# Keeping the first loads in the written order, and adding the last w_down tiles to r in SBUF

## The chip, the cores and the metric

One core of one Trainium2 chip runs the kernel. The metric is the device time of one execution in microseconds (us), as the median of several runs. Beside it stands one profiled execution, whose span (first to last instruction) is a little shorter than its device time.

## The reference

One decoder layer on 256 tokens and 2048 channels, all in fp32. Cut to what matters here:

```python
h = rms_norm(r, g_mix);  z = h @ w_in                      # 2048 -> 3072 (q, k, v) + 3072 (conv) + 4096 (gates)
q, k, v = split(z)                                         # 8 heads of 128, q and k normalised per head
attn = softmax(causal(q k^T)) v;  y_attn = attn @ w_attn_out
y_conv = (c_b * conv3(c_c * c_x)) @ w_conv_out
r = r + (sigmoid(g_a) * y_attn + sigmoid(g_c) * y_conv) @ w_o
r = r + relu(rms_norm(r, g_mlp) @ w_up)**2 @ w_down        # 2048 -> 8192 -> 2048
r = r + sigmoid(rms_norm(r, g_ple) @ w_ple_gate) * (p @ w_ple_proj)
```

## The kernel before, in words

Every weight is read once from DRAM in fp32 and split by ScalarE (ACT) and VectorE (DVE) into a high and a low part (`w_hi`, `w_lo`), as the activations are; three products of parts (high by high, high by low, low by high) on TensorE (PE) make one fp32 product. All 277 MB of weights go through this, so the kernel is one long row of products on PE with splits ahead of it and loads ahead of the splits.

The stages, in order of time:

- **The first chunks** (`first_chunks`): q, k and v of heads 0 to 3. The sum over 2048 channels goes in 16 steps of 128; in each step 256 KB of weights for each of q, k and v (`raw_first`) and 128 KB of x (loaded in pairs of steps, 256 KB) come in, are split, and enter 18 products of 512 columns. This function is written out in its order of work: `ordered[0] = True` marks each of its instructions, the loads too, to be kept in program order on its engine.
- **The second q, k, v chunk** (`rows(qkv(1), ...)` and so on, tiles `raw`): four units of 1 MB for each of q, k, v, and 24 products for each. After each unit one entry of the list `pending` is run (`run_pending`). The attention of head 0 to 7 is put there in four stages each: transposes of q and k (`tr_qk`), scores and softmax, transposes of the probabilities, values.
- **conv, gates, branches, w_o**, then **up and down** (96 units `g`): 64 units of w_up and 32 of w_down. Half of w_down's output goes through the loop's own products (`ps_dn`), the other half through a scheme of seven products per block (`P1` to `P7`).
- **The gate** (`ps_pg`), 16 tiles, with the projection of p.

The order of the instructions on each engine comes from a scheduler that runs when the kernel is built. An instruction that is not kept in program order may be put ahead of others as soon as its buffer is free. The loads of the second q chunk (`raw`, four buffers) are not kept in order. All these loads are issued by SyncE (SP), with at most eight DMAs of SP and ACT under way: each waits for the eighth one before it, and the load of the vector `vec` from ACT's queue is one of the eight.

The residual r lies in SBUF only until the norm ahead of up is taken; a copy in DRAM (`r_kept`, eight tiles of two column blocks) is kept, and GpSimd (POOL) adds the finished tiles of `ps_dn` to it by DMAs that accumulate (`dn_done`, two for each tile `n`, both into the same block, so that the second waits for the first). Towards the end r is loaded back by `load_r`. The last four tiles of w_down (`n` of 12 to 15 with `q` 3) are added by DVE in SBUF. In unit 95 ACT takes r in blocks 10 to 14 into the gate's input (`enter_high`), and only behind them on ACT stand the copies out of the banks `P1` and `ps_dn` (tiles `p1` and `dn`); the copy `dn` frees the bank that the first gate product needs.

Of the kernel before, what the change touches and what calls it, by code (L numbers as in the profile page):

```python
# [12 lines left out]
ALU = mybir.AluOpType  # L13
# [6 lines left out]
S = 256  # L20
# [18 lines left out]
def hybrid_block_kernel(ctx: ExitStack, tc: tile.TileContext, ins: dict, out: bass.AP):  # L39
# [9 lines left out]
    nc = tc.nc  # L49
# [8 lines left out]
    def slot(shape, dtype, name):  # L58
        return bp.tile(shape, dtype, tag="slot", name=name)
# [4 lines left out]
    def psum(kind, shape, name):  # L64
        i = banks[kind].pop(0)
        banks[kind].append(i)
        return pp.tile(shape, F32, tag=f"b{i}", name=name)

    def bank(name):
        return psum("acc", [P, CW], name)  # L70


    ordered = [False]

    def inorder(ins):
        return tc.keep_in_program_order(ins) if ordered[0] else ins

    def act(*args, **kw):
        return inorder(nc.scalar.activation(*args, **kw))  # L79

    def mm(*args, **kw):
        return inorder(nc.tensor.matmul(*args, **kw))  # L82

    def load(*args):
        return inorder(nc.sync.dma_start(*args))

    class vec_ops:
        def __getattr__(self, name):
# [29 lines left out]
    def rsqrt_mean(dst, sumsq, n, k):  # L118

        dve.tensor_scalar(dst, sumsq, 1.0 / n, EPS, op0=ALU.mult, op1=ALU.add)  # L120
        nc.gpsimd.tensor_tensor(dst, dst, half[:, :k], op=ALU.pow)
# [23 lines left out]
    pending = []  # L145

    def run_pending(n):
        for _ in range(min(n, len(pending))):
            pending.pop(0)()
# [37 lines left out]
    def rows(units, xs, name, pops=1):  # L187

        nu = len(units)
        ps = [bank(f"ps_{name}_{t}") for t in range(NT)]  # L190
        for u, unit in enumerate(units):
            wt = unit()
            for j in range(KU):
                k = KU * u + j
                hi, lo = (p[:, (j % 2) * CW:(j % 2 + 1) * CW] for p in wt[j // 2])
                for t in range(NT):
                    xh, xl = (xs[k][:, i, t * P:(t + 1) * P] for i in range(2))
                    mm(ps[t], xh, hi, start=k == 0, stop=False)
                    mm(ps[t], xh, lo, start=False, stop=False)
                    mm(ps[t], xl, hi, start=False, stop=k == KU * nu - 1)  # L200
            run_pending(pops)
        return ps

    def qkv(c, loader=load_unit):
        return [lambda u=u: loader(ins["w_qkv"][c, u]) for u in range(4)]
# [60 lines left out]
    def rstd_rows(rstd, name):  # L266
        diag = slot([P, NT, P], F32, f"diag_{name}")
        for t in range(NT):
            dve.tensor_scalar_mul(diag[:, t, :], ident, rstd[:, t:t + 1])
        ps = psum("tr", [P, S], f"ps_rstd_{name}")  # L270
        mm(ps, ones, diag.rearrange("p t s -> p (t s)"), start=True, stop=True)
        row = const.tile([P, S], F32, tag="rstd_row", name=f"rstd_row_{name}")
        act(row, ps, AF.Copy)
        return row


    xT, st0, xraw = {}, {}, {}
# [76 lines left out]
    qs, ks, vs = {}, {}, {}  # L354

    def tokens(ps, name):

        parts = []
        for t in range(NT):
            raw = slot([P, CW], F32, f"{name}_{t}")  # L360
            act(raw, ps[t], AF.Copy, scale=st0["col"][:, t:t + 1])
            parts.append(raw)
        return parts

    def qk_evac(ps, name):
        parts = tokens(ps, name)
        ssq = sm.tile([P, NT, 4], F32, tag="ssqh", name=f"ssq_{name}")
        for t in range(NT):
            junk = sm.tile([P, HD], F32, tag="junk", name="junk", bufs=1)
            for h in range(4):  # L370
                act(junk, parts[t][:, h * HD:(h + 1) * HD], AF.Square, accum_out=ssq[:, t, h:h + 1])
        rinv = sm.tile([P, NT, 4, 1], F32, tag="rinvh", name=f"rinv_{name}")
        rsqrt_mean(rinv.rearrange("p t h o -> p (t h o)"), ssq.rearrange("p t h -> p (t h)"), HD, NT * 4)
        for t in range(NT):
            heads = parts[t].rearrange("p (h d) -> p h d", d=HD)
            dve.tensor_mul(heads, heads, rinv[:, t].to_broadcast([P, 4, HD]))
        return parts
# [51 lines left out]
    for c in range(2):  # L429
        if c == 0:  # L430
            ps_q, ps_k, ps_v = first_chunks((0, 2, 4), ("q0", "k0", "v0"))
            qs[c], ks[c] = qk_evac(ps_q, "q0"), qk_evac(ps_k, "k0")
            vs[c] = tokens(ps_v, "v0")
        else:
            qs[c] = qk_evac(rows(qkv(1), xT, "q1"), "q1")
            ks[c] = qk_evac(rows(qkv(3), xT, "k1"), "k1")
            vs[c] = tokens(rows(qkv(5), xT, "v1"), "v1")
        for h in range(4 * c, 4 * c + 4):
            head(h)
        if c == 0:  # L440
            pending.insert(4, lambda: st0.update(row=rstd_rows(st0["col"], "mix")))


    w_in = ins["w_in"]
# [2 lines left out]
    for j in range(8):  # L447
# [5 lines left out]
        u = slot([P, S + 2], F32, f"u_{j}")  # L453
# [27 lines left out]
    for c in range(4):  # L481
        gates = []
        for i in range(2):
            ps = rows(tiles("w_in", 24 + 16 * i + 4 * c), xT, f"g{i}_{c}", pops=2)
            g = [slot([P, CW], F32, f"g{i}_{c}_{t}") for t in range(NT)]
# [14 lines left out]
    r = {}  # L500

    def add_to_r(n, src):

        dst = r[n // 2][:, n % 2, :]
        for i in range(2):
            dve.tensor_add(dst, src[:, i * S:(i + 1) * S], dst)
# [6 lines left out]
    r_kept = [dram.tile([P, 2, S], F32, tag=f"r{u}", name=f"r_kept_{u}") for u in range(8)]  # L513
# [43 lines left out]
    def stages(g):  # L557
        return staged[g] if 0 <= g < len(staged) else ()
# [131 lines left out]
    def up_sum(k, st):  # L690
        a = u_raw[k] = temp("a")
        dve.tensor_add(a, st[:, :S], st[:, S:])
        dve.scalar_tensor_tensor(a, a, 0.0, row1, op0=ALU.max, op1=ALU.mult)
# [27 lines left out]

    def dn_done(q, n, st):
        if q < 3 or n < 12:
            for i in range(2):
                nc.gpsimd.dma_start(r_kept[n // 2][:, n % 2, :], st[:, i * S:(i + 1) * S], accum_op=ALU.add)  # L725
        else:
            add_to_r(n, st)

    def load_r(u):
        r[u] = slot([P, 2, S], F32, f"r_{u}")  # L730
        nc.gpsimd.dma_start(r[u], r_kept[u])
# [7 lines left out]
    for g in range(NU):  # L739
        kind, i = units[g]  # L740
        ordered[0] = g > 1
        if g == 5:
            banks["acc"] = [7]
        load_raw(g + 3)
        for j, x in stages(g + 2):
            if x == 0:
                load_pair(j)
        for u in {88: (6, 7), 90: (0, 1), 91: (4,), 92: (2, 3), 93: (5,)}.get(g, ()):
            load_r(u)
        if g == 93:  # L750
            ss2 = slot([P, 2, S], F32, "ss2")
        if g == 94:
            praw = slot([P, 2, S], F32, "p")
            load(praw, ins["pT"].rearrange("p (k s) -> p k s", s=S))
        xs = hT if kind == "up" else {k: uT[16 * i[0] + k] for k in range(16)}
        ps = cols(wU[g][1:], xs, f"{kind}_{g}")
        if g == 0:
            rstd1 = rstd_columns(ss1, "mlp")
        if g == 1:
            row1 = rstd_rows(rstd1, "mlp")  # L760
        done = [n for n in range(g) if n in evac] if g > 1 else []
        ups = [units[n][1] for n in done if units[n][0] == "up"]
        on_act, on_dve = unit_half(g + 2, 0)
        on_act()
        for n in done:
            if units[n][0] == "up":
                up_sum(units[n][1], evac.pop(n))
        on_dve()
        for k in ups:
            up_high(k)  # L770
        for k in ups:
            up_low(k)
        for n in done:
            if units[n][0] == "dn":
                dn_done(*units[n][1], evac.pop(n))
        make_stages(stages(g))
        for work in unit_half(g + 2, 1):
            work()
        entering = {94: (8, 9), 95: (10, 11, 12, 13, 14)}.get(g, ())
        for n in entering:  # L780
            enter_high(n)
            if n % 2 == 1:
                square(n // 2)
        if g == NU - 1:
            p1 = evacuated(prod["P1"], "p1")
        for n in entering:
            enter_low(n)
        if g == NU - 1:
            d, e = (slot([P, CW], F32, n) for n in "de")
            dve.tensor_sub(d, p1, prod["P5"])  # L790
            dve.tensor_add(e, d, prod["P3"])
        evac[g] = evacuated(ps, kind)
        if kind == "up" and i == 63:
            up_sum(i, evac.pop(g))
            up_high(i)
            up_low(i)
        for j, x in stages(g - 1):
            products(j, x)
# [186 lines left out]
```

## Time and profile before

| | |
|---|---|
| device time, median of 3 runs | 1460.81 us (1459.35 to 1461.93) |
| the profiled execution, device time | 1459.0 us |
| its span | 1457.2 us |
| PE busy | 1439.0 us, 99% of the span |
| DVE busy | 1057.6 us, 73% |
| ACT busy | 822.4 us, 56% |
| POOL busy | 70.3 us, 5% |
| moved by DMA | 289.95 MB, mean 199 GB/s |
| mean granted TensorE clock | 0.999 of full speed |

1.8 us of the profiled execution lie outside its span. A busy PE is not always one at its full rate: its matmuls overlap, their ends are modelled, and the clock can be granted at half.

### The profile page before, as it was taken

Reading aid. Unit: us, or ns where it says so; the run is one execution under the profiler, and the core shown is the slowest. Engines: PE = TensorE matmul, PEld = TensorE weight load, DVE = VectorE, ACT = ScalarE, POOL = GpSimd, SP = SyncE. Lnnn points to the kernel's source line nnn. Section 1 sums busy time; section 2 is a strip of 40 time slices with the busy share of each in tenths; the row PEclk is TensorE's granted clock in tenths of the full one; section 3 lists DMA queues with packets and bytes.
Section 4 is the critical chain, followed back from the end, with each engine's and each line's share of the span. In section 5 each row is a group of like instructions: output and inputs, shape, how many; then the busy total and the mean of one; then the engine's idle time right before and its main releaser. Section 6 shows DMA issues by size and latency. Waiting matters only on the chain.

```text
span 1457.2 us, 19838 instructions
## 1 busy us (share of the span) xinstructions
PE 1439.0 (99%) x7553; PEld 1235.7 (85%) x7553; DVE 1057.6 (73%) x1616; ACT 822.4 (56%) x1291; POOL 70.3 (5%) x99
## 2 busy tenths in 40 slices
PE   7999999999999999999999999999999999999998
PEld 5878888888888888888888888888888888887887
DVE  5755677755555646676889788887888879987984
ACT  4766555554444444445666566665666556655752
POOL 0010000000000000000001100021000200011000
PEclk9999999999999999999999999999999999999999
DMA  9755554555555666563658865697557866578470
GB/s 299 248 176 174 173 174 174 173 190 194 195 183 194 201 213 225 202 216 126 229 178 229 214 218 181 198 238 222 190 181 225 238 183 220 198 229 238 150 248 22
DMA packets 139375, 289.95 MB, mean 199 GB/s; under 512 B 8208, under 2 KB 83216, under 8 KB 119056
## 3 DMA queue, kind: packets, MB, share of 16 engines
q1 hardware_dynamic: 129792, 277.11, 57.0%
q0 software_dynamic: 9344, 11.54, 4.7%
q8 instruction: 59, 0.97, 0.3%
q14 instruction: 36, 0.29, 0.1%
q10 hardware_dynamic: 144, 0.04, 0.0%
HBM read 277.12 MB, written 11.53 MB: 198 GB/s over the span
## 4 chain that ended last, share of the span: by engine, by line
PE 96%; ACT 1%; DMA 1%; DVE 1%; issue 0%; POOL 0%; SPq 0%; DVEq 0%; ACTq 0%
PE ps_up L82 24%; PE ps_g L82 12%; PE ps_dn L82 12%; PE P L82 10%; PE ps_conv L82 9%; PE ps_o L82 6%; PE ps_pg L82 6%; PE ps_y L82 6%; PE ps_q L82 3%; PE ps_k L82 3%; PE ps_v L82 3%; PE ps_proj L82 1%; DMA x<-in_xT_dram 1%; DMA r<-r_kept 0%; ACT w_hi L79 0%; PE tr L470 0%
## 5 line engine op out<-in xcount | busy, mean ns | idle before, releaser
L89 DVE TENSOR_TENSOR w_lo<-raw,w_hi 128x1024 fp32r<-128x1024 f32 (+1 forms) x524 | 529.0, 1026 | 233.4 <-ACT w_hi L79 170.4
L79 ACT ACTIVATE w_hi<-raw 128x1024 fp32r<-128x1024 f32 (+1 forms) x524 | 459.2, 895 | 216.1 <-PE ps_g L82 62.0
L82 PE MATMUL ps_up<-x,w_hi 128*128 128x512 f32 x1024 | 254.5, 391 | 0.4 <-ACT up L79 0.4
L82 PEld LDWEIGHTS ps_up<-x,w_hi 128*128 128x128 f32 x1024 | 191.1, 188 | 40.5 <-ACT up L79 3.6
L82 PE MATMUL ps_g<-w_hi,x 128*128 128x512 f32 x512 | 159.1, 390 | 0.0
L82 PEld LDWEIGHTS ps_up<-x,w_lo 128*128 128x128 f32 x1024 | 131.3, 191 | 5.0
L82 PE MATMUL ps_up<-x,w_lo 128*128 128x256 f32 x1024 | 132.8, 283 | 0.0
L82 PE MATMUL ps_dn<-x,w_hi 128*128 128x512 f32 x512 | 126.8, 390 | 0.0
L82 PEld LDWEIGHTS ps_g<-w_hi,x 128*128 128x128 f32 x512 | 96.2, 188 | 19.8
L82 PEld LDWEIGHTS ps_dn<-x,w_hi 128*128 128x128 f32 x512 | 96.2, 188 | 18.9 <-ACT dn L79 0.3
L79 ACT ACTIVATE t_hi<-t 128x1024 fp32r<-128x1024 f32 x64 | 67.5, 1054 | 72.2 <-DVE t L89 72.2
L79 ACT ACTIVATE up<-ps_up 128x512 f32<-128x512 f32 x64 | 38.2, 597 | 119.2 <-PE ps_up L82 119.1
L82 PE MATMUL ps_g<-w_lo,x 128*128 128x512 f32 x256 | 99.7, 389 | 0.0
L82 PE MATMUL ps_conv<-x,w_hi 128*128 128x512 f32 x384 | 97.9, 398 | 0.0
L89 DVE TENSOR_TENSOR t_lo<-t,t_hi 128x1024 fp32r<-128x1024 f32 x64 | 78.1, 1220 | 16.7 <-ACT t_hi L79 16.7
L82 PEld LDWEIGHTS ps_conv<-x,w_hi 128*128 128x128 f32 x384 | 70.9, 189 | 13.3
L82 PE MATMUL ps_y<-w_hi,x 128*128 128x512 f32 x256 | 79.5, 389 | 0.0
L725 POOL DMA_DIRECT2D r_kept<-dn x56 | 48.4, 887 | 523.0 <-ACT dn L79 376.9
L82 PE MATMUL ps_pg<-x,w_hi 128*128 128x512 f32 (+1 forms) x272 | 68.1, 383 | 3.2 <-ACT dn L79 3.2
L82 PE MATMUL P<-t_hi,s 128*128 128x512 f32 x192 | 70.6, 395 | 0.0
L82 PEld LDWEIGHTS ps_dn<-x,w_lo 128*128 128x128 f32 x512 | 65.7, 191 | 2.5
L82 PE MATMUL ps_dn<-x,w_lo 128*128 128x256 f32 x512 | 66.4, 283 | 0.0
(206 smaller groups left out, 2133.9 us busy)
## 6 DMA issues: line engine op xcount, KB each, us to landing
raw<-in_w_up_dram SPq DMA_DIRECT2D x64, 1024.0 KB, 5.3
raw<-in_w_in_dram SPq DMA_DIRECT2D x56, 1024.0 KB, 5.0
raw_s<-in_w_down_dram SPq DMA_DIRECT2D x128, 256.0 KB, 4.3
raw<-in_w_down_dram SPq DMA_DIRECT2D x32, 1024.0 KB, 5.1
raw<-in_w_branch_dram SPq DMA_DIRECT2D x16, 1024.0 KB, 5.1
raw<-in_w_o_dram SPq DMA_DIRECT2D x16, 1024.0 KB, 4.9
raw<-in_w_qkv_dram SPq DMA_DIRECT2D x12, 1024.0 KB, 5.0
raw_first<-in_w_qkv_dram SPq DMA_DIRECT2D x48, 256.0 KB, 7.2
```

Source lines behind the costliest of these rows:

```text
L79: return inorder(nc.scalar.activation(*args, **kw))
L82: return inorder(nc.tensor.matmul(*args, **kw))
L89: return lambda *args, **kw: inorder(getattr(nc.vector, name)(*args, **kw))
L725: nc.gpsimd.dma_start(r_kept[n // 2][:, n % 2, :], st[:, i * S:(i + 1) * S], accum_op=ALU.add)
```

## The change

Two things. First, loads are also kept in program order until the four units of the second q chunk have been written (`ordered_loads`), and an entry that does nothing is put ahead of the attention's first stage in `pending`, so that all stages are run one unit later. Second, the DMAs that add the tiles 8 to 11 of the last quarter of w_down accumulate into the tile r in SBUF instead of `r_kept`, and r's blocks 4 to 7 are loaded back ahead of them, in unit 88.

```diff
+    ordered_loads = [True]
+
     def load(*args):
-        return inorder(nc.sync.dma_start(*args))
+        dma = nc.sync.dma_start(*args)
+        return tc.keep_in_program_order(dma) if ordered[0] or ordered_loads[0] else dma
...
-            qs[c] = qk_evac(rows(qkv(1), xT, "q1"), "q1")
+            ps_q = rows(qkv(1), xT, "q1")
+            ordered_loads[0] = False
+            qs[c] = qk_evac(ps_q, "q1")
...
-            pending.insert(4, lambda: st0.update(row=rstd_rows(st0["col"], "mix")))
+            pending.insert(0, lambda: None)
+            pending.insert(5, lambda: st0.update(row=rstd_rows(st0["col"], "mix")))
...
     def dn_done(q, n, st):
         if q < 3 or n < 12:
+            to = r_kept if q < 3 else r
             for i in range(2):
-                nc.gpsimd.dma_start(r_kept[n // 2][:, n % 2, :], st[:, i * S:(i + 1) * S], accum_op=ALU.add)
+                nc.gpsimd.dma_start(to[n // 2][:, n % 2, :], st[:, i * S:(i + 1) * S], accum_op=ALU.add)
...
-        for u in {88: (6, 7), 90: (0, 1), 91: (4,), 92: (2, 3), 93: (5,)}.get(g, ()):
+        for u in {88: (4, 5, 6, 7), 91: (0, 1), 92: (2, 3)}.get(g, ()):
             load_r(u)
```

SP, the queue that issues the loads, at the start of the program, before and then after. `raw` are units of the second q chunk (1 MB), `raw_first` and `x_0` pieces of the first step (256 KB and 128 KB):

```order
L85 DMA raw_783<-in_w_qkv_dram 128x2048
L85 DMA raw_825<-in_w_qkv_dram 128x2048
L85 DMA raw_873<-in_w_qkv_dram 128x2048
L85 DMA raw_first_114<-in_w_qkv_dram 128x512
L85 DMA x_0_116<-in_xT_dram 128x256
L85 DMA raw_first_118<-in_w_qkv_dram 128x512
```

```order
L88 DMA raw_first_114<-in_w_qkv_dram 128x512
L88 DMA x_0_116<-in_xT_dram 128x256
L88 DMA raw_first_118<-in_w_qkv_dram 128x512
L88 DMA raw_first_120<-in_w_qkv_dram 128x512
L88 DMA x_0_116<-in_xT_dram 128x256
```

The three units of 1 MB have left the head of the queue, and a fourth its middle; all four now stand right behind the last `raw_first`, and behind the second chunk's twelve units SP's rows are the same as before.

PE in the second q chunk, at the first of the attention's stages, before and then after (`ps_q` are the products of the chunk, `tr_qk` the transposes of q and k of head 0):

```order
L82 MATMUL ps_q_1_782<-w_hi,x 128x512
L389 MATMUL tr_qk_817<-ident,q_0_737 128x128
L389 MATMUL tr_qk_817<-ident,q_1_739 128x128
L82 MATMUL ps_q_0_781<-w_hi,x 128x512
L389 MATMUL tr_qk_817<-ident,k_0_757 128x128
```

```order
L82 MATMUL ps_q_1_782<-w_hi,x 128x512
L393 MATMUL tr_qk_851<-ident,q_0_737 128x128
L393 MATMUL tr_qk_851<-ident,q_1_739 128x128
L393 MATMUL tr_qk_851<-ident,k_0_757 128x128
L393 MATMUL tr_qk_851<-ident,k_1_759 128x128
```

Before, the transposes stood behind the first 24 products of the chunk, now they stand behind 48.

POOL from unit 88 to 93, before and then after (`r_kept` is the copy in DRAM, `r_4` to `r_7` the tiles in SBUF, `dn` a finished tile of w_down):

```order
L731 DMA r_6_11730<-r_kept_6_4733 128x512
L731 DMA r_7_11732<-r_kept_7_4734 128x512
L725 DMA r_kept_4_4731<-dn_11791 128x256 x2
L731 DMA r_0_11876<-r_kept_0_4727 128x512
L731 DMA r_1_11878<-r_kept_1_4728 128x512
L725 DMA r_kept_4_4731<-dn_11862 128x256 x2
L731 DMA r_4_11959<-r_kept_4_4731 128x512
L725 DMA r_kept_5_4732<-dn_11939 128x256 x2
L731 DMA r_2_12032<-r_kept_2_4729 128x512
L731 DMA r_3_12034<-r_kept_3_4730 128x512
L725 DMA r_kept_5_4732<-dn_12018 128x256 x2
L731 DMA r_5_12111<-r_kept_5_4732 128x512
```

```order
L739 DMA r_4_11730<-r_kept_4_4731 128x512
L739 DMA r_5_11732<-r_kept_5_4732 128x512
L739 DMA r_6_11734<-r_kept_6_4733 128x512
L739 DMA r_7_11736<-r_kept_7_4734 128x512
L733 DMA r_4_11730<-dn_11795 128x256 x2
L733 DMA r_4_11730<-dn_11866 128x256 x2
L739 DMA r_0_11959<-r_kept_0_4727 128x512
L739 DMA r_1_11961<-r_kept_1_4728 128x512
L733 DMA r_5_11732<-dn_11939 128x256 x2
L739 DMA r_2_12034<-r_kept_2_4729 128x512
L739 DMA r_3_12036<-r_kept_3_4730 128x512
L733 DMA r_5_11732<-dn_12020 128x256 x2
```

The load of `r_5` has moved from behind the accumulates into block 5 to ahead of all of them; the last of POOL's DMAs is now an accumulate.

## Rows read from the trace of the kernel before

**Rows 1.** Waits of PE over the whole span (us in total, times, longest):

```profile
PE ps_q L82 <- DVE x L89: 7.4, 1, 7.4
PE ps_pg L82 <- ACT dn L79: 3.2, 1, 3.2
PE tr_qk L389 <- DVE k L89: 1.7, 1, 1.7
```

**Rows 2.** Timeline, 0 to 40 us (start, length, engine, line, operation, [idle before, releaser]):

```profile
0.74 1.34 SPq L85 DMA_DIRECT2D raw<-in_w_qkv_dram  x3
1.19 4.02 PE L82 MATMUL idle<-zero 128*128 128x512 bf16 x9 [1.19 <-DVE half L89]
...
12.07 0.35 DVE L89 TENSOR_SCALAR x<-x,vec 128x256 fp32r<-128x256 f32 x1 [10.92 <-DMA x<-in_xT_dram]
...
12.57 1.19 PE L82 MATMUL ps_q<-w_hi,x 128*128 128x512 f32 x2 [7.36 <-DVE x L89]
...
17.61 0.63 PE L82 MATMUL ps_v<-w_hi,x 128*128 128x512 f32 x2
```

**Rows 3.** Chain that ended last, 0 to 160 us (start, length, what):

```profile
2.86 9.11 DMA x<-in_xT_dram
...
12.57 2.90 PE ps_q L82 x6
...
19.16 1.36 PE ps_q L82 x6
...
125.15 5.47 PE ps_k L82 x24
```

**Rows 4.** DMA view, issues of 0 to 2 us, then queues of 3 to 3.5 us:

```profile
vec<-in_vec_dram ACTq DMA_DIRECT2D x1, 37.0 KB, 5.4
...
q1 hardware_dynamic: 23, 0.19, 89.0%
q10 hardware_dynamic: 23, 0.01, 5.7%
```

**Rows 5.** Windows: length, busy time (instructions) per engine, granted clock, DMA share, GB/s:

```profile
5.21:12.57 7.36, 0.00 (x1) 0.03 (x1) 0.50 (x2) 0.63 (x1) 0.00 (x0) 1.00 1.01 379
19.16:64.04 44.88, 44.88 (x200) 37.18 (x199) 35.65 (x64) 32.70 (x61) 0.00 (x0) 1.00 0.96 295
155.00:1300.00 1145.00, 1144.55 (x6061) 986.87 (x6060) 846.07 (x1282) 644.85 (x960) 51.85 (x70) 1.00 0.63 199
1344.03:1347.22 3.19, 0.00 (x0) 0.00 (x0) 2.32 (x6) 3.14 (x7) 0.00 (x0) 1.00 0.00 0
1347.22:1353.00 5.78, 5.62 (x25) 4.76 (x26) 5.61 (x11) 1.98 (x3) 0.00 (x0) 0.70 0.00 0
```

**Rows 6.** Timeline of SP at the end of the first chunks:

```profile
53.34 5.47 SPq L85 DMA_DIRECT2D raw_first<-in_w_qkv_dram  x6
```

**Rows 7.** Timeline, second q and k chunk: PE's first product, DVE's softmax end, ACT's copies:

```profile
81.15 0.39 PE L82 MATMUL ps_q<-w_hi,x 128*128 128x512 f32 x1
...
128.33 0.55 DVE L89 TENSOR_SCALAR s<-s,den 128x128 f32<-128x128 f32 x2
...
131.99 1.26 ACT L79 ACTIVATE k<-ps_k,rstd_mix 128x512 f32<-128x512 f32 x2
```

**Rows 8.** Timeline of POOL, from 1280 us:

```profile
1288.44 0.88 POOL L725 DMA_DIRECT2D r_kept<-dn  x1 [22.15 <-ACT dn L79]
...
1294.50 1.44 POOL L731 DMA_DIRECT2D r<-r_kept  x2
...
1330.51 0.86 POOL L725 DMA_DIRECT2D r_kept<-dn  x1 [6.75 <-DMA r_kept<-dn]
1336.49 0.58 POOL L731 DMA_DIRECT2D r<-r_kept  x1 [5.12 <-DVE x L89]
```

**Rows 9.** Tile dn from 1270 us: landing of its eight accumulating DMAs:

```profile
DMA to landing us min/median/max: 3.6/7.2/8.0
```

**Rows 10.** Timeline of ACT, unit 95:

```profile
1335.64 2.00 ACT L79 ACTIVATE w_hi<-raw 128x1024 fp32r<-128x1024 f32 x2
1343.07 0.91 ACT L79 ACTIVATE x<-r,vec 128x256 fp32r<-128x256 f32 x2 [5.43 <-DMA r<-r_kept]
```

## The prediction

> **What bounds the kernel now.** I read first what PE waited for, since PE is busy 99% of the span: only three waits of any size stand there, 7.4 us before the first `ps_q`, 1.7 us at `tr_qk` and 3.2 us before `ps_pg` [rows 1]. Then the windows, to see whether time won early would be lost in the middle: from 155 to 1300 us PE is busy for 1144.55 of 1145.00 us [rows 5]. A late start or a late end cannot be made up there, and an early one is passed on, as long as loads and splits keep the pace that PE sets; the DMA engines are at 0.63 in that stretch. So each of the three waits counts in full, and the change touches all three. Then the timeline and the chain around each.
>
> At the start SP issues three units of 1 MB first, from 0.74 us on [rows 2]. The first piece of x is issued only at 2.86 us and lands 9.11 us later, at 11.97 us [rows 3]; DVE and PE start right on it, at 12.07 and 12.57 us [rows 2]. Between 5.21 and 12.57 us the DMA engines are full and move 379 GB/s, and PE does nothing [rows 5]. The reader is to see that this is data of a later stage: the second chunk's first product runs at 81.15 us [rows 7].
>
> At the end ACT waits 5.43 us for the load of r and takes x from it at 1343.07 us [rows 10]. POOL issued this load at 1336.49 us, after the accumulates into `r_kept` that must have landed before it, the last of them issued at 1330.51 us [rows 8]. Behind these instructions on ACT stands the copy `dn` that PE waits for.
>
> **The change part by part: the start.** It removes three transfers of 1.05 MB from the head of the queue: 3.15 MB at 379 GB/s [rows 5] are 8.3 us. The first x would land near 11.97 - 8.3 = 3.7 us. It needs `vec` too, whose load took 5.4 us from its issue at about 0.74 us, so until 6.1 us. That is an upper bound. In the half microsecond from 3 us its queue q10 and SP's q1 moved 23 packets each [rows 4], q1's packets of 0.19 MB / 23 = 8 KB: small packets and large ones took turns. With rows of 2 KB (256 KB over 128 rows) in place of 8 KB the turns are about a fourth as long, so I estimate `vec` by about 4.2 us. Then x is scaled (0.35 us [rows 2]) and is ready before the nine idle products end, at 1.19 + 4.02 = 5.21 us [rows 2]. I take the first real product at 5.2 us in place of 12.57; with `vec` at 6.1 us it would be 6.6 us.
>
> A second term lies in the pace. The first six products took 2.90 us (0.48 each), later six take 1.36 us (0.227 each) [rows 3]; the slow pairs last until about 17 us, and at 17.61 us a pair takes 0.63 us [rows 2]. The idle products ran at 4.02 / 9 = 0.45 us. So PE ran at the lower of its two levels (1.2 and 2.4 GHz) after standing still for 7.36 us, although the clock column reads 1.00 before it: the duration decides, not the column. The step of 18 products took from 12.57 to 19.16 us, 6.6 us in place of 3 x 1.36 = 4.1: 2.5 us lost. Now real products come straight behind 4.02 us of idle ones. The bounds are a loss of 0 and of 2.5 us; I take 0.4, near the first, because it was the pause that stood ahead of the slow stretch, and it goes. So step 1 would start at 5.2 + 4.1 + 0.4 = 9.7 us where it started at 19.16 [rows 3]: **9.4 us**. With `vec` late and the slow pace kept it is 6.6 + 6.6 = 13.2 us, a gain of 5.9; with no loss at all, 9.9.
>
> What hides the rest: a step brings 3 x 262 + 131 = 917 KB, at 295 GB/s [rows 5] in 3.1 us, and PE uses 4.1 us for it. ACT and DVE are busy for 32.70 and 35.65 of 44.88 us [rows 5], so they keep up too. The page "SBUF — State Buffer" of the Trainium skill, section "The DMA setup-cost knee", speaks against this change: each transfer pays a fixed cost, and one of 256 KiB reaches 224 GB/s where 1 MiB reaches 341. By that figure a step takes 917 / 224 = 4.1 us to load, just PE's own pace, and the first chunks would hang on the loads. The 295 GB/s with pieces of that size in flight say that they overlap, and decide.
>
> The four units of the second chunk lose their early start. SP issued the last piece of the first chunks at about 53.34 + 5.47 = 58.8 us [rows 6], now near 49.4. Four units are 4.19 MB, 14.2 us at 295 GB/s, so all have landed by 64 us and the first by some 54; PE needs the first at 81.15 - 9.4 = 71.8 us [rows 7]. The cover is over 15 us; if it were gone, the first unit's 3.6 us would be the price.
>
> **The transposes.** PE waited 1.7 us at `tr_qk` for the normalised k [rows 1]. One unit later means 24 products or 5.47 us later [rows 3], so 3.8 us remain to spare: **1.7 us**. All later stages of the attention slip by one unit. For head 1 the softmax now meets the copies of the second k. Before, DVE ended it at 128.33 + 0.55 = 128.9 us [rows 7], and PE's products covered until 125.15 + 5.47 = 130.6 [rows 3]: 1.7 us to spare. Two copies ahead of it take 1.26 us [rows 7]. It still fits; if it didn't, some tenths each.
>
> **The end.** Accumulating into r makes the load of `r_5` early and leaves an accumulate last. I follow POOL's new order from the first accumulate at 1288.44 us [rows 8]: the second of each tile waits for the first, which lands after 7.2 us [rows 9]; there are four such waits and the last landing, 5 x 7.2 = 36 us, and between them three issues of 0.88 us and two pairs of loads of 1.44 us [rows 8], 5.5 us. Block 5 is complete at 1330 us, with the longest landing, 8.0 us [rows 9], at 1334. No row shows an accumulate that ends in SBUF; loads of r and accumulates are the nearest, and I take the accumulates' own landing. ACT reaches block 5 at 1335.64 + 2.00 = 1337.6 us [rows 10], so the wait goes, and the copy `dn` comes before PE is done with the last `P`, at 1344.03 us. That gives 3.2 us [rows 5], and more: behind the pause the granted clock was 0.70 for 5.78 us [rows 5]. At two levels, 1.00 and 0.50, that is 0.6 x 5.78 = 3.5 us at half rate, 1.7 us lost, and 0.16 us more of PE idle lie there. Sum **5.0 us**; if DVE's chain behind it (additions from P1 to P7) holds PE up, 3.2. The four loads in unit 88 need buffers early; they stand ahead of the first accumulate, which waited 22.15 us idle [rows 8] for its tile, and that is their cover.
>
> On the landing: the page "DMA: Bandwidth & Descriptors" of the Trainium skill, section "Anatomy of one DMA", says that most of a transfer's fixed cost is the wait for the confirmed write, longest where it goes to HBM. By it the new accumulates land sooner than 7.2 us, and the slack of 7.6 us grows; no run here shows it yet, and the sum stays.
>
> **Sum.** 9.4 + 1.7 + 5.0 = 16.1 us. The profiled execution took 1459.0 us, which makes 1442.9; it lies 1.8 us under the median of the runs, 1460.8, which would make 1444.7. I say 1443.9, between the two.
>
> **Rivals.** (1) The first step stays slow, or `vec` is late: PE's pace does not care for the idle products. For it speaks that all of them ran slowly. The gain at the start is 7.3 (slow pace alone) to 5.9 us, the time 1446 to 1447.5. (2) Block 5 is late still: accumulates into SBUF of 9 us or more each. The end's 5 us are lost, 1449. (3) The start is given back: the first chunks hang on the loads, as the first page's figure has it, or the second chunk waits for its units. The start's 9.4 us shrink to 2 or so, 1451. Against it stand 295 GB/s and the 15 us of cover. (4) Slower: the chain of accumulates grows so long that PE waits longer than all that is won before. The load of r ended ACT's wait at 1343.07 us [rows 10]; adding 9.4 + 1.7 gives 1354.2 as the point from which it decides, so 12.1 us for each of the five landings: (1354.2 - 1288.44 - 5.5) / 5. At 13 us each the time would be 1464. The longest seen is 8.0 [rows 9]. (5) It does not do what it says: the first x lands as late as now, because the DMA engines start slowly and not because of the three units; then 1453 from the other two terms.
>
> **Chances.** My forecast 0.68, its own range 1441.5 to 1446. (1) 0.14, (2) 0.06, (3) 0.07, (4) 0.02, (5) 0.03. The range must leave out no more than 2 in 10: it reaches over the first two rivals to 1450, and down to 1441.0 for a start and end at their upper bounds. A measurement here can tell about 0.2%, 2.9 us, from no change. All cases but (4) win more than that: faster 0.95, same 0.03, slower 0.02.
>
> **What would show it.** In the profile after: the first `ps_q` at about 5 us, no pause between the idle products and it, the first 18 products in little over 4.1 us, the second chunk's first product near 72 us, no wait at `tr_qk`, the last accumulate landed well before ACT's x in unit 95, PE without a pause before `ps_pg` and a granted clock of 1.00 there. I am wrong if PE waits for `w_hi` or `x` in steps 1 to 4, if the first products take 0.48 us each, if a wait of PE on POOL's DMA remains at the end, or if pauses appear between 155 and 1300 us that weren't there.

## The result, and the profile after

The changed kernel took 1444.34 us (median of 4 runs, 1443.79 to 1445.12), the kernel before 1460.08 (4 runs, 1457.51 to 1461.93): a ratio of 0.9894, 95% interval 0.9877 to 0.9911. The forecast was 1443.9 us, within 1441.0 to 1450.0. The profiled execution after took 1445.12 us with a span of 1443.3, the one before 1459.0, so the two traces differ by 13.9 us where the medians differ by 15.7. All that follows explains the 13.9.

What PE waited for after (line, releaser; us in total, times, longest); [rows 1] are the three longest of the same list of before:

```profile
PE idle L82 <- DVE half L93: 1.2, 1, 1.2
PE ps_up L82 <- ACT up L79: 0.4, 1, 0.4
PE ps_rstd_mix L82 <- DVE diag_mix L93: 0.4, 1, 0.4
PE tr_qk L393 <- DVE k L93: 0.3, 1, 0.3
```

The three waits of before, 12.3 us, are gone but for 0.3 us at `tr_qk`, and a new one of 0.4 stands at `ps_rstd_mix`. (`ps_ss_mix` sums the squares of x for the first norm; `rstd_mix` is the norm's factor, begun on DVE and finished on POOL; `ps_rstd_mix` lays it out along a row.) To see where the time came from, I read from both timelines of PE when it starts the same product; the difference is the time won up to there.

| start of | before, us | after, us | won |
|---|---|---|---|
| first `ps_q` | 12.57 | 5.36 | 7.21 |
| step 1 of the first chunks | 19.00 | 10.23 | 8.77 |
| step 2 | 23.08 | 14.94 | 8.14 |
| `ps_ss_mix` (48 products before the end of the first chunks) | 69.32 | 61.18 | 8.14 |
| second chunk, first product | 81.15 | 73.01 | 8.14 |
| first `ps_g` (attention and conv are over) | 299.72 | 290.97 | 8.75 |
| last `ps_dn` | 1341.34 | 1332.70 | 8.64 |
| first `ps_pg` | 1347.22 | 1335.22 | 12.00 |
| `ps_ss_ple` | 1370.48 | 1356.61 | 13.87 |
| last product's end | 1453.04 | 1439.17 | 13.87 |

So the start brought 8.1 us, the stretch from the second chunk to the first `ps_g` 0.6, and the end 5.2; in between 0.1 was lost. The timeline of the start (start, length, engine, line, operation, idle before and releaser):

```profile
1.19 4.02 PE L82 MATMUL idle<-zero 128*128 128x512 bf16 x9 [1.19 <-DVE half L93]
5.36 1.19 PE L82 MATMUL ps_q<-w_hi,x 128*128 128x512 f32 x2
...
6.17 0.63 ACT L79 ACTIVATE w_hi<-raw_first 128x512 fp32r<-128x512 f32 x1 [1.30 <-DMA raw_first<-in_w_qkv_dram]
...
6.35 0.83 PE L82 MATMUL ps_q<-w_lo,x 128*128 128x512 f32 x2
...
7.02 0.63 PE L82 MATMUL ps_q<-w_hi,x 128*128 128x512 f32 x2
...
7.69 0.63 ACT L79 ACTIVATE w_hi<-raw_first 128x512 fp32r<-128x512 f32 x1 [0.89 <-DMA raw_first<-in_w_qkv_dram]
...
11.12 1.30 ACT L79 ACTIVATE w_hi<-raw_first 128x512 fp32r<-128x512 f32 x2 [1.61 <-DMA raw_first<-in_w_qkv_dram]
...
11.80 0.73 PE L82 MATMUL ps_k<-w_hi,x 128*128 128x512 f32 x2
...
12.53 0.73 PE L82 MATMUL ps_k<-w_lo,x 128*128 128x512 f32 x2
```

Read it against [rows 2]: the first real products stand directly behind the idle ones, and only two pairs are slow (1.19 and 0.83 us) before one takes 0.63. Step 0 takes 4.87 us where 18 products at full pace take 4.1. ACT waits for pieces of weights there, but PE does not: its products follow each other without a pause, so the slow pairs are the difference. Step 1 takes 4.71 us. There the piece of k's weights comes late, ACT waits for it until 11.12 us, and the products that use it start only at 11.80 and 12.53. In step 1 the loads hold PE, for 0.6 us.

Windows of after (length, busy time and instructions of PE, PEld, DVE, ACT, POOL, granted clock, DMA share, GB/s), for the first step, the stretch behind the first `ps_pg` and the middle:

```profile
5.21:9.70 4.49, 4.34 (x17) 3.57 (x17) 2.81 (x7) 1.90 (x3) 0.00 (x0) 1.00 0.93 260
1335.22:1341.00 5.78, 5.78 (x36) 5.05 (x35) 5.64 (x10) 2.84 (x6) 0.00 (x0) 1.00 0.02 4
155.00:1300.00 1145.00, 1144.56 (x6063) 986.46 (x6062) 850.23 (x1285) 644.77 (x958) 54.74 (x74) 1.00 0.63 201
```

The first row shows 260 GB/s at a share of 0.93: the DMA engines are nearly full. The second row answers to the last of [rows 5]: no pause ahead of it and a clock of 1.00 where it was 0.70. The third is the middle, as full as before.

The second chunk, from the timeline:

```profile
60.09 2.01 ACT L79 ACTIVATE w_hi<-raw 128x1024 fp32r<-128x1024 f32 x2 [1.41 <-DMA raw<-in_w_qkv_dram]
...
61.18 0.95 PE L82 MATMUL ps_ss_mix<-ones,ss 128*128 128x1 f32 x8
61.18 3.71 DVE L93 TENSOR_TENSOR w_lo<-raw,w_hi 128x1024 fp32r<-128x1024 f32 x3 [1.70 <-ACT w_hi L79]
...
64.81 0.15 DVE L93 TENSOR_SCALAR rstd_mix<-ps_ss_mix 128x2 f32<-128x2 f32 x1
64.88 1.22 DVE L93 TENSOR_TENSOR w_lo<-raw,w_hi 128x1024 fp32r<-128x1024 f32 x1
...
65.05 1.61 POOL L125 TENSOR_TENSOR rstd_mix<-rstd_mix,half 128x2 f32<-128x2 f32 x1 [62.58 <-DVE rstd_mix L93]
...
83.45 1.29 DVE L93 TENSOR_TENSOR k<-k,rinv_k 128x512 f32<-128x512 f32 x2 [1.53 <-POOL rinv_k L125]
...
84.90 0.30 PE L393 MATMUL tr_qk<-ident,k 128*128 128x128 f32 x1 [0.30 <-DVE k L93]
```

`ps_ss_mix` is done at 62.1 us, but DVE takes it up (`rstd_mix`) only at 64.81, since three splits of raw units stand ahead, and the first of these units landed late: ACT waited for it until 60.09. Everything up to the normalised k hangs on `rstd_mix`. Before, the three splits were done by the time `ps_ss_mix` was, and DVE took it up at once; the same two rows of DVE there:

```profile
70.31 0.16 DVE L89 TENSOR_SCALAR rstd_mix<-ps_ss_mix 128x2 f32<-128x2 f32 x1 [0.22 <-PE ps_ss_mix L82]
...
88.07 1.29 DVE L89 TENSOR_TENSOR k<-k,rinv_k 128x512 f32<-128x512 f32 x2 [1.53 <-POOL rinv_k L121]
```

The end, from the timelines of POOL, ACT and PE, and below it the landing of the eight accumulating DMAs (min, median, max):

```profile
1279.80 0.89 POOL L733 DMA_DIRECT2D r<-dn  x1 [16.26 <-ACT dn L79]
...
1312.74 0.88 POOL L733 DMA_DIRECT2D r<-dn  x1 [5.43 <-DMA r<-dn]
...
1328.89 0.89 ACT L79 ACTIVATE x<-r,vec 128x256 fp32r<-128x256 f32 x2
...
1335.22 1.52 PE L82 MATMUL ps_pg<-x,w_hi 128*128 128x512 f32 x6
```

```profile
DMA to landing us min/median/max: 3.5/6.2/7.8
```

The last accumulate is issued at 1312.74, so block 5 is complete near 1318.9 us; ACT comes to it at 1328.89 and waits for nothing. That is 10 us to spare. PE begins `ps_pg` straight behind the last `P`.

### The profile page after: what moved, and what is told of

Its sections match the earlier page's. It is cut to its first block, busy times and chain, and to the rows that moved or that the text cites. A ratio compares the mean times of both kernels' runs of the same rounds, so it can differ in the third digit from the quotient of the medians.

```text
span 1443.3 us, 19851 instructions
## 1 busy us (share of the span) xinstructions
PE 1436.6 (100%) x7553; PEld 1232.9 (85%) x7553; DVE 1057.8 (73%) x1616; ACT 822.4 (57%) x1291; POOL 71.2 (5%) x99
## 4 chain that ended last, share of the span: by engine, by line
PE 92%; DMA 4%; ACT 2%; DVE 1%; issue 0%; POOL 0%; SPq 0%; ACTq 0%; DVEq 0%; POOLq 0%
PE ps_up L82 24%; PE ps_dn L82 12%; PE ps_g L82 12%; PE P L82 11%; PE ps_conv L82 9%; PE ps_o L82 7%; PE ps_pg L82 6%; PE ps_y L82 6%; DMA raw_first<-in_w_qkv_dram 2%; PE ps_v L82 2%; DMA x<-in_xT_dram 1%; DMA raw<-in_w_qkv_dram 1%; PE ps_k L82 1%; PE ps_q L82 1%; PE ps_proj L82 1%; ACT w_hi L79 1%
## 5 line engine op out<-in xcount | busy, mean ns | idle before, releaser
L733 POOL DMA_DIRECT2D r_kept<-dn x48 | 41.1, 877 | 476.2 <-ACT dn L79 351.9
```

The costliest lines, as they stand in the source:

```text
L733: nc.gpsimd.dma_start(to[n // 2][:, n % 2, :], st[:, i * S:(i + 1) * S], accum_op=ALU.add)
```

## Experiments

Times are medians of the runs named. "Won at `ps_ss_mix`" and the like are differences of PE's starts against the profiled execution of before, as in the table above.

**Only the order of the loads**, on the kernel before:

```diff
+        dma = nc.sync.dma_start(*args)
+        return tc.keep_in_program_order(dma) if ordered[0] or ordered_loads[0] else dma
...
+            ps_q = rows(qkv(1), xT, "q1")
+            ordered_loads[0] = False
```

> Only the order of the loads is changed. Theory A (read from the trace after): the early start is worth 8.1 us up to the second chunk's first product, and then the raw units of the second chunk, which now land late, put the normalised k some 3.5 us late against PE; with the transposes still in their old place the wait at tr_qk grows from 1.7 to about 5 us. Net about 4.7 us faster than before, a profiled time near 1454. Rival B (the late units delay nothing that PE waits for; the small waits of the trace after come from the moved transposes): tr_qk stays at 1.7 us, net 8.1 us, near 1451. The end is as before in both: about 3.2 us of wait before ps_pg.

1455.33 us (8 runs, 1452.13 to 1456.66) beside 1460.03 of the kernel before (22 runs, 1454.70 to 1463.53), ratio 0.9965 (0.9951 to 0.9978). It won 9.0 us at `ps_ss_mix` and had 3.1 left at the first `ps_g`. Its two longest waits of PE, and its windows around and behind the first of them:

```profile
PE tr_qk L392 <- DVE k L92: 5.7, 1, 5.7
PE ps_pg L82 <- ACT dn L79: 3.0, 1, 3.0
```

```profile
81.00:84.00 3.00, 0.07 (x1) 0.10 (x2) 1.47 (x3) 0.26 (x1) 2.06 (x1) 0.56 0.83 292
84.00:87.00 3.00, 3.00 (x9) 2.31 (x10) 1.52 (x2) 0.84 (x2) 0.00 (x0) 0.50 0.38 115
87.00:90.00 3.00, 3.00 (x12) 2.43 (x11) 0.01 (x1) 1.06 (x1) 0.00 (x0) 0.80 0.79 317
```

Theory A holds, and its price was too low: the wait grew to 5.7 us, and PE, once it had stood still, came back at the lower level (a clock of 0.50, then 0.80 in a window that holds the rise), which costs some 2 us more. Alone, this part gives back two thirds of what it wins.

**Only the moved transposes**, on the kernel before:

```diff
-            pending.insert(4, lambda: st0.update(row=rstd_rows(st0["col"], "mix")))
+            pending.insert(0, lambda: None)
+            pending.insert(5, lambda: st0.update(row=rstd_rows(st0["col"], "mix")))
```

> Only the transposes of the first heads are moved by one unit. Theory A: the wait of 1.7 us at tr_qk goes and nothing comes in its place, since with the old order of loads the raw units land early and 3.8 us of cover remain: 1.7 us faster, profiled near 1457.3, PE waits at tr_qk and ps_rstd_mix of 0.1 us or less. Rival B: the move itself brings the waits of 0.3 us at tr_qk and 0.4 at ps_rstd_mix that the changed kernel shows: 1.0 us faster, with these two waits in PE's list.

1456.66 us (10 runs, 1452.25 to 1460.16), ratio 0.9984 (0.9968 to 0.9999). The wait at `tr_qk` is gone and `ps_rstd_mix` shows 0.4 us: half of each theory. The move itself brings the wait at `ps_rstd_mix`, and not the one at `tr_qk`. From `ps_ss_mix` to the first `ps_g` this kernel won 1.3 us (1.7 less 0.4); its first chunks ended 0.6 us later than before, so 0.7 are left there, and 1.8 at the end, where the wait before `ps_pg` was 2.5 us. By the ratio it won 2.3 us, hardly more than the scatter of these kernels. Its trace also holds a row that the one of before lacks, the granted clock at the start:

```profile
8.00:11.00 3.00, 0.00 (x0) 0.00 (x0) 0.00 (x0) 0.00 (x0) 0.00 (x0) 0.55 0.98 394
11.00:14.00 3.00, 1.44 (x4) 1.18 (x5) 1.67 (x4) 1.26 (x2) 0.00 (x0) 0.50 0.97 242
```

While PE stands and waits for x, the clock falls to the lower level, and the first products run at it. The prediction inferred this from durations, against a column that read 1.00.

**Loads and transposes, without the part on r:** both edits above.

> Order of the loads and place of the transposes, without the part on r. If the parts add up: 8.1 + 0.6 us to the end of the attention, 8.7 us faster than before, profiled near 1450.3, and at the end the old wait of 3.2 us before ps_pg and the old stretch with a clock of about 0.7. Rival: the end of the kernel depends on when the work reaches it (its loads and accumulates meet other transfers after an earlier start), then the wait before ps_pg differs from 3.2 us by more than 0.5.

1449.65 us (4 runs, 1447.76 to 1450.43), ratio 0.9925 (0.9903 to 0.9946). Won 8.35 us at the first `ps_g`. Loads alone left 3.07 there and the move alone 0.74: in these executions the two together are worth 4.5 us more than their sum, and by the three ratios 3.5 (each known to 2 or 3 us), since the move is what lets most of the early start through. Its waits of PE at `tr_qk`:

```profile
PE tr_qk L392 <- ACT w_hi L79: 0.9, 1, 0.9
PE tr_qk L392 <- DVE k L92: 0.3, 1, 0.3
```

That is 1.2 us where the changed kernel, whose work is the same up to there, waited 0.3. (In the first row the profile names a split of ACT, which ended last; the transposition needs k, and DVE had normalised it only 0.15 us before the product began.) The wait before `ps_pg` was 2.5 us in place of 3.2, a little beyond the margin of the rival. But it was 2.5 with the move alone too, where the work arrived only 0.8 us earlier, and 3.0 with the loads alone, where it arrived 3.2 us earlier. That the end depends on when the work arrives is not shown.

**Only the part on r**, on the kernel before:

```diff
+            to = r_kept if q < 3 else r
...
-        for u in {88: (6, 7), 90: (0, 1), 91: (4,), 92: (2, 3), 93: (5,)}.get(g, ()):
+        for u in {88: (4, 5, 6, 7), 91: (0, 1), 92: (2, 3)}.get(g, ()):
```

> Only the part on r: 5.2 us faster than before, profiled near 1453.8; the wait before ps_pg goes from 3.2 to under 0.1 us and the clock behind it from 0.70 to 1.00 (1.7 us of the 5.2). Rival: the changed kernel's gain at the end came partly from its earlier start; then 3.2 us or less and a clock under 1.00 remain here.

1455.31 us (9 runs, 1454.17 to 1457.50), ratio 0.9964 (0.9952 to 0.9975). In the profiled execution it lagged 3.1 us behind the kernel before at the last `ps_dn` and led by 2.1 at the end: the part on r is worth 5.2 us, with no wait before `ps_pg`. The lag has nothing to do with r, since all of it is there at the first `ps_g`. Its two longest waits of PE:

```profile
PE ps_q L82 <- DVE x L89: 7.5, 1, 7.5
PE tr_qk L389 <- DVE k L89: 4.0, 1, 4.0
```

The wait at `tr_qk` was 4.0 us in this execution and 1.7 in the one of before, with the same loads and the same order there; behind it the granted clock was 0.64 and 0.80 in two stretches of 3 us. The first chunks ended 0.7 us earlier, the three splits later, and `rstd_mix` fell behind them. So the wait that the change removes has no fixed size, and the late units are one way to lengthen it, not the only one.

**One idle product in place of nine**, on the changed kernel (`range(9)` becomes `range(1)`):

> The changed kernel with one idle product ahead of the first real one in place of nine. Theory A (PE's pace at the start follows from what it did just before): the first products take about 0.48 us each for some microseconds instead of one slow pair, step 1 starts later by up to 2.5 us less what the loads hide (steps 0 and 1 waited for loads anyway), so 1 to 2 us slower than the changed kernel. Rival B (the slow pace belongs to the first microseconds of the program and not to the pause): no change in the first products, same time within 0.3 us.

One run, 1445.54 us. From its timeline:

```profile
6.36 1.05 PE L82 MATMUL ps_q<-w_lo,x 128*128 128x512 f32 x2
...
9.77 1.05 PE L82 MATMUL ps_k<-w_hi,x 128*128 128x512 f32 x2
...
11.72 0.62 PE L82 MATMUL ps_v<-w_hi,x 128*128 128x512 f32 x2
```

```profile
63.50 0.16 DVE L93 TENSOR_SCALAR rstd_mix<-ps_ss_mix 128x2 f32<-128x2 f32 x1 [0.90 <-PE ps_ss_mix L82]
63.81 1.22 DVE L93 TENSOR_TENSOR w_lo<-raw,w_hi 128x1024 fp32r<-128x1024 f32 x1
63.74 0.71 POOL L125 TENSOR_TENSOR rstd_mix<-rstd_mix,half 128x2 f32<-128x2 f32 x1 [61.27 <-DVE rstd_mix L93]
```

The slow pairs of 1.05 us last until near 11 us, as they lasted until near 17 in [rows 2]. So the pace of the first step follows from what PE did just before it, theory A, and the idle products are worth 1.3 us at `ps_ss_mix` against the changed kernel's profiled execution, 1.7 to 2.2 against the seven others with these loads and nine idle products. At the end only 0.4 of the 1.3 is left, less than expected: with PE later, `rstd_mix` comes directly after `ps_ss_mix`, and the wait at `tr_qk` vanishes.

**The transposes one unit later still**, on the changed kernel:

```diff
             pending.insert(0, lambda: None)
-            pending.insert(5, lambda: st0.update(row=rstd_rows(st0["col"], "mix")))
+            pending.insert(0, lambda: None)
+            pending.insert(6, lambda: st0.update(row=rstd_rows(st0["col"], "mix")))
```

> The changed kernel with the transposes of the first heads moved by one unit more. Theory A (after the change rstd_mix stands on VectorE behind three splits of late raw units, which ate the 3.8 us that the first move left): the waits of 0.3 us at tr_qk and 0.4 at ps_rstd_mix go, 0.7 us faster than the changed kernel, profiled near 1444.4. Rival B: the move pushes the last heads' work against the convolution and the wait comes up there; no gain, or 1 us slower. The difference is below what the times alone can tell, so PE's list of waits and the milestones of the two traces decide.

1443.41 us (6 runs, 1443.19 to 1443.77), ratio to before 0.9893 (0.9876 to 0.9910). Both waits are gone and a wait of 0.2 us at `tr_p` is new; between `ps_ss_mix` and the first `ps_g` it won 0.8 us on the changed kernel. I timed it again, with the changed kernel beside it on one chip.

> The changed kernel itself once more, beside the next kernel on the same chip. 1443.8 to 1445.2 us as before; in the trace the first chunks end (ps_ss_mix) between 60.3 and 61.2 us, as in the six kernels with these loads, and PE waits 0.3 to 1 us in all at tr_qk and ps_rstd_mix.

> The transposes moved by one unit more, timed again beside the changed kernel on one chip. Theory A (the 0.7 to 0.8 us that its trace won between the first chunks and the convolution are real): 0.6 to 1.2 us under the changed kernel's median, with ranges that hardly touch. Rival B (it was the scatter of the first chunks, whose end moved by 0.9 us between the two profiled runs): the medians lie within 0.3 us of each other.

The changed kernel: 1444.91 us (4 runs, 1444.50 to 1445.11), `ps_ss_mix` at 60.69. The further shift: 1443.56 (4 runs, 1443.18 to 1443.96), `ps_ss_mix` at 60.29. The ranges don't touch, 1.35 us lie between the medians and 1.3 between the spans of the two traces, a little above what theory A allowed; 0.4 of it is the scatter of the first chunks and some 0.9 the shift. It is the fastest kernel of this study, by 0.09%. From `ps_ss_mix` to the first `ps_g` its three executions (one of them in the last experiment below) won 1.4 us each on the one of before; in the five with the changed kernel's start it was between a loss of 0.3 and a gain of 1.3. The shift takes out a wait whose size varies. Its waits of PE in the second execution, besides those at `idle` and `ps_up`:

```profile
PE tr_p L419 <- DVE s L93: 0.2, 1, 0.2
PE ps_q L82 <- DVE x L93: 0.2, 1, 0.2
```

**A longer chain of accumulates**, on the changed kernel:

```diff
+            if q == 3 and n == 11:
+                for _ in range(2):
+                    nc.gpsimd.dma_start(to[5][:, 1, :], nought, accum_op=ALU.add)
```

> The changed kernel with two accumulates of zeros more on the block r_5, behind the last of the real ones; nothing is left out. Theory A (the chain of accumulates is off the path with about 10 us to spare: the last one was issued at 1312.74 us, lands 6.2 us later, and ScalarE comes to the block at 1328.9): two more links of 6.2 us and 0.9 us of issue are 14 us, 4 us more than there is to spare, so a wait of about 4 us before ps_pg, and the granted clock falls under 1.00 behind it: 4 to 6 us slower than the changed kernel. Rival B (the landing is not what ScalarE waits for, or the links overlap): under 1 us slower.

One run, 1446.27 us, and the trace ends 1.1 us later than that of the changed kernel. ACT's and PE's timelines, PE's wait, and the landing of the two accumulates:

```profile
1330.96 0.51 ACT L79 ACTIVATE x<-r,vec 128x256 fp32r<-128x256 f32 x1 [1.88 <-DMA r<-nought]
...
1337.66 0.51 ACT L79 ACTIVATE x<-r,vec 128x256 fp32r<-128x256 f32 x1 [2.98 <-DVE r L93]
...
1338.22 0.39 PE L82 MATMUL ps_pg<-x,w_lo 128*128 128x256 f32 x1 [0.94 <-ACT x L79]
```

```profile
PE ps_pg L82 <- ACT x L79: 0.9, 1, 0.9
```

```profile
DMA to landing us min/median/max: 5.1/5.6/6.1
```

Theory A's mechanism shows, its price was too high: ACT now does wait for the landing, so the 10 us to spare are real. But two links took 11.5 us and not 14 (I had counted the issue beside the landing that contains it), and of ACT's 1.9 us only 0.9 reach PE. They come by a longer way than theory A had it: ACT's copy `p` stands behind that x, DVE's additions to r stand behind `p`, and PE waits for the x of a later block that ACT takes from their sum. No fall of the clock is recorded behind the pause of 0.9 us, yet PE went from 0.3 us ahead of the changed kernel at the first `ps_pg` to 1.1 behind.

**Tiles 8 to 11 of the last quarter added by DVE** in place of the accumulating DMAs, on the changed kernel (`if q < 3 or n < 12:` becomes `if q < 3:`):

> The changed kernel with the tiles 8 to 11 of the last quarter added by VectorE, as tiles 12 to 15 are, in place of the accumulating transfers. Theory A (the accumulates are hidden and so would VectorE's additions be): the time is the same within 0.5 us, with no wait before ps_pg. Rival B (VectorE's additions delay its copies or splits that PE waits for): slower by 1 us or more with new waits of PE on VectorE in the last 100 us.

One run, 1443.79 us. From the first `ps_g` on it gains 0.3 us on the changed kernel, and no wait before `ps_pg` appears. DVE hides these additions (0.87 us for a tile), as POOL's DMAs hide theirs: theory A.

**Two of the first weight pieces issued by POOL**, on the kernel with the further shift:

```diff
+            if k < 2 and c == 1:
+                nc.gpsimd.dma_start(raw[k, c], src)
```

> The kernel with the further shift, and two of the first six weight pieces (those of k in steps 0 and 1) are issued by POOL instead of SP. Theory A (steps 0 and 1 hung on the transfers, whose DMA engines were at 0.93 and moved 260 GB/s, not on SP's issuing): no gain, step 1 starts at 9.5 to 10.3 us as before, the time within 0.5 us. Rival B (SP's issue of 0.45 us each, one behind the other, holds the pieces up): the two pieces land a microsecond earlier, steps 0 and 1 take 4.1 us each, 0.7 to 1.2 us faster. A third possibility is that POOL's queue lands later: then step 0 takes over 5 us.

1445.08 us (4 runs, 1444.94 to 1445.27), 1.5 us slower than the same kernel without it. It is the third possibility: POOL issues both pieces by 3.74 us, but step 0 stretches from 5.31 to 11.63 us.

```profile
PE ps_k L82 <- ACT w_hi L79: 1.5, 1, 1.5
```

```profile
raw_first<-in_w_qkv_dram POOLq DMA_DIRECT2D x2, 256.0 KB, 6.8
```

A second queue only let other pieces pass the one that PE needed next: POOL issued the piece of k of step 0 at 2.42 us and it landed at 7.79; without the second queue SP issued it at 1.65 and it landed at 5.97. Since POOL's issue came later than SP's, the run does not settle whether SP's issuing holds the first steps.

## Why the prediction was right, point by point

**What bounds the kernel: right.** PE's three waits were the whole of it, the middle passed the gain on (8.75 us won at its beginning, 8.64 at its end).

**The start: right in its mechanism, 1.3 us too large (9.4 against 8.1).** The first product came at 5.36 us (said: 5.2) and `vec` landed at 4.4 us (said: about 4.2). The 1.3 us have three parts.

- Reading, 0.3 us: the first product was 0.16 us late, and the sum lets step 1 of before begin at 19.16 us, where the piece of the chain begins; by PE's timeline it began at 19.00.
- The slow pace, 0.4 us: it cost 0.8 us in step 0 (said: 0.4).
- One wait in step 1, 0.6 us, where the sum had nothing. What failed is the sentence that hides the loads: "a step brings ... 917 KB, at 295 GB/s in 3.1 us, and PE uses 4.1". The rate is not the reason. At the 260 GB/s of the first step 917 KB take 3.5 us (an estimate from that row), still less than PE's 4.1. But at the very start nothing lies ready ahead of PE, so a single late piece is a wait: the piece of k of step 1 was issued at 3.54 us and landed at 11.10; with only the loads changed it was issued at 3.54 too, landed at 9.95, and step 1 took 4.08 us.

Neither the slow pace nor the wait has a fixed size. In the eight profiled executions with these loads and nine idle products, the slow pace was over after none to four products, step 0 took 4.6 to 5.1 us, and step 1 took 4.1 us in five of them and 4.4 to 4.7 in three. Where the first products ran at full pace, step 0 still took 4.6 to 4.7 us, with short stops for splits of the weights. The eight won 8.1 to 9.0 us at `ps_ss_mix`, so the profiled one lay at the low end, and 9.4 is over all of them.

The page "SBUF — State Buffer" of the Trainium skill, section "The DMA setup-cost knee", which the prediction set against the change, would have the loads at PE's own pace. The trace does not bear it out: the first step moved 260 GB/s against the page's 224 for one such transfer, and from step 2 on every step of the eight executions took PE's own 4.1 us.

**The transposes: a third of the gain came (0.6 against 1.7).** The step that failed is "so 3.8 us remain to spare". It took for granted that k is ready as long after the first chunks as before. From the start of `ps_ss_mix` to the start of k's normalising it took 18.8 us in the three executions where `rstd_mix` came directly behind it (before, the move alone, one idle product), and 19.9 to 23.6 in the others, where splits on DVE came between; 22.3 in the changed kernel. Of these 3.5 us more, 2.7 are DVE's splits, and the rest is POOL's operation on `rstd_mix`, which took 1.61 us in place of 0.71. That alone is less than 3.8. But k comes in two halves, and the transposition of the second, which stood two products behind that of the first, now stands directly behind it; it is the second for which PE waited, 0.3 us. The size varies here too: with the same work up to there, the waits at `tr_qk` were 0.5 us in the changed kernel's second execution, 1.2 without the part on r, and none with DVE's additions. A further 0.4 is the wait at `ps_rstd_mix`, which belongs to the move and which the prediction did not see; some 0.4 of longer busy time in the same stretch I did not follow further. In rival (3) the second chunk's units were to make PE itself wait. The first four landed at 60.0 to 67.4 us (said: 54 to 64), PE still never waited for a split of them, and the lateness travelled over DVE's order instead.

**The end: right (5.0 against 5.2).** The wait of 3.2 us went, the clock stayed at 1.00 as the sum had it, and block 5 was complete 10 us ahead of ACT (said: 7.6). The lone part on r repeated the 5.2, and the longer chain showed where the 10 us end. Accumulates into SBUF landed after 6.2 us in the median, into DRAM after 7.2 [rows 9]. The page "DMA: Bandwidth & Descriptors" of the Trainium skill, section "Anatomy of one DMA", says that the confirmed write weighs most where it goes to HBM; these two medians agree, by 1.0 us. The size is not shown, though: in the four executions with accumulates into DRAM the median was 6.3 to 7.2 us, in the eight with accumulates into SBUF 5.9 to 6.4, and the transfers beside them were not the same.

**The sum.** 16.1 us against 13.9 in the profiled pair. That the forecast lay within 0.5 us of the median is partly luck: it stood between the profiled execution and the median of before, and the medians moved by 15.7.

**The rivals.** (1) The slow pace would have stayed without the idle products, as the kernel with one of them showed; with nine it was over after four products at most. (2) and (4) are excluded by 10 us to spare. (3) holds in small, as above: loads took 0.6 us of the start in the profiled execution, and the late units' splits ahead of `rstd_mix` some tenths of the transposes. (5) The first x landed at 4.8 us; the three units had been what delayed it.

## What to carry to other kernels

A mean transfer rate says little about the first steps, in which nothing lies ready ahead: cost these apart, piece by piece, by when each lands and when it is needed. When a change makes one engine earlier, follow the order on the other engines too, since the instruction that is late next can be a small one behind others in a queue (`rstd_mix` behind three splits). And a part that seems worth little alone can be what lets another one through: here the moved transposes won 1.3 us by themselves, and with the loads the two won 4.5 us more than their sum (3.5 by the ratios of the times). Last, a wait read from one execution can have another size in the next: look at several before a sum leans on its tenths.

## What the runs showed of the hardware beyond this

- **A pause can cost more than its length.** In the kernel with only the loads PE stood still for 5.7 us, and the granted clock was 0.50 and 0.80 in the next two rows of its windows; in the kernel with only the part on r it stood for 4.0 us, with 0.64 and 0.80 behind it; with the longer chain it stood for 0.9 us and the column stayed at 1.00, yet the kernel lost 1.4 us there. The record of the clock can miss a stretch: in the trace of before the column read 1.00 at the start, in that of the moved transposes 0.50 at the same place, with products of the same length.
- **The changed kernel scatters less.** The kernel before ran from 1454.70 to 1463.53 us over 22 runs, the changed one from 1443.79 to 1445.12 over two sets of 4. The wait at `tr_qk`, 1.7 and 4.0 us in two executions of the same piece of program, is one source, but it does not explain the whole: the kernel with only the moved transposes had no such wait in its profiled execution, and ran from 1452.25 to 1460.16 us over 10 runs. What else scatters stays open.
- **POOL's small operation on `rstd_mix`** took 0.71 us in the three executions where it began ahead of DVE's next split (one idle product, before, the move alone), and 1.61 us in the changed kernel, where a split of 1.22 us had begun on DVE at 64.88 us, 0.17 us before it. The page "SBUF — State Buffer" of the Trainium skill, section "SBUF: two separate sides", says that VectorE with two inputs and GpSimd take a port from each other as a whole, and that the first to start has it; POOL's rows agree. DVE's do not show the other direction: in the kernel with one idle product the split at 63.81 us, which began while POOL's operation ran, took 1.22 us all the same.
